# Gathered second product four tokens wide, with a ring of nine buffers, in an encoder layer with a mixture of small experts

## Chip, core and metric

One core of a Trainium2 chip runs the whole program in one launch. The metric is the device time of the launch in microseconds, the median of three runs. The engines of the core are TensorE (PE in the rows; PEld is its weight load), VectorE (DVE), ScalarE (ACT), GpSimd (POOL) and SyncE (SP); each executes its own instructions in the order in which they were built into the program, and waits on semaphores for the others. SP, ACT and POOL issue transfers to 16 DMA engines, which they share.

## What is computed

One encoder layer is applied to a prompt of 256 tokens and a sample of 1024, both 1024 features wide, in float32. Two branches (a gated linear recurrence and a latent attention) are merged and added to the input. Then each token picks 128 of 16384 experts (8 heads, the 16 best of each), and its output is the sum over its experts:

```python
u = jnp.take(u_tab, eidx, axis=0)
ve = jnp.take(v_tab, eidx, axis=0)
act = jax.nn.gelu(jnp.einsum('td,thkd->thk', zt, u).astype(jnp.float32), approximate=False) * g
return jnp.einsum('thk,thkd->td', act.astype(zt.dtype), ve)
```

Here `zt` is the normed token, `g` the softmax over its picks. A closing norm follows. `u_tab` and `v_tab` have 16384 rows of 1024 float32 numbers, 4 KB a row.

## The kernel before

Tokens go by tiles of 128. There are two prompt tiles and eight sample tiles. For six of the ten tiles (both of the prompt, the sample's first two, `r0`, and its last two, `r1`) the experts' rows are gathered; for the four sample tiles between them (`ND` = 512 tokens) all 16384 experts are computed, those not picked with weight zero (`dense`).

A gathered tile takes 256 gathers. One gather brings 128 rows, one to each partition, 512 KB in all, as an indirect DMA issued by GpSimd.

- First product (`u_steps`, L933 and L935): gather s brings every token's row of its slot s; VectorE multiplies it by the normed token `zs` and sums over the features (`dots`). 128 gathers a tile. Behind them come the gelu and the weights (`act`).
- Second product by tokens (`v_steps`, L946 to L978), for the prompt's tiles and the sample's first: gather t brings all 128 rows of one token, and TensorE contracts them over the partitions with that token's activations. The activations are transposed first (L949). A token t = 32 g + i writes into column group g of the array (`tile_position=(0, g_ * 32)`) and adds into its own row of `acc`; the weights are zero in the other 31 columns (`zt`). Each token takes two matmuls of 512 columns, and two tokens of neighbouring groups are handed over together (`VG = 2`).
- Second product by slots (`v_slots`, L989 and L991), for `r0[1]` and both of `r1`: gather s brings every token's row of slot s, and VectorE multiplies it by the activation and adds it to `vacc`.

All these rows land in one ring of five buffers of 4 KB a partition (`tag="ring", bufs=5`), in the order in which they are asked for; the n-th gather waits until VectorE or TensorE is through with the gather five before it. The two vectors `gfin` and `gffn`, gains of the closing norm and of the norm in front of the experts, lie in buffers of their own, loaded once.

`experts(routes)` interleaves a tile's first product with the second product of the tile before it, one step each in turn. It is called for the two prompt tiles while the sample's projection, recurrence and attention run, and for `r0 + r1` while the rest of the sample's attention, its merge and then `dense` run.

The stages around it are `attn_core` for the sample (L138 `kt,qt`, L618, L624), `merge` for the sample's first two tiles and then the other six (wo products, L140 `msh,wh`; wq products, L138 `xg,wraw`; the picks on VectorE in `best` and `half`, closed by a transpose in `finish_picks`, L892 or L912), `weights` (L1024, L1043) and `dense`. `dense` walks over 128 blocks of 128 experts: `first(b)` loads a block of u, splits it in two float32r parts (`uh` on ScalarE, `ul` on VectorE, L124), makes three products for each of 8 slices (L140 to L142, `zth,uh`), a gelu, a multiplication by the picks' weights (`ge`, L1072), and a split of the result; `second(g)` does the same with v for four blocks at a time (`vl`, L124), and VectorE adds the products to `acc` (L1086).

The order of instructions on each engine isn't written out by hand. The framework's scheduler sets it when the program is built, from dependencies, priorities and a simulated timeline (`schedule_with_timeline_sim=True`); the steps of the second products are issued with high priority. `dense` and `experts` are written one after the other, and the scheduler merges them. Part of each partition's memory is set aside for the descriptors of transfers that GpSimd issues, 16384 bytes unless said otherwise.

Of the kernel before, what the change touches and what calls it, by code (L numbers as in the profile page):

```python
# [12 lines left out]
F32 = mybir.dt.float32  # L13
# [25 lines left out]
VG = 2  # L39
# blocks of the input projection, 128 columns each  # L40
B_Q, B_FF, B_FB, B_I, B_G, B_CQ, B_CKV, B_GLH, B_GLA, B_PE = 0, 4, 8, 12, 16, 20, 23, 25, 33, 41
# columns of the gains
# [8 lines left out]
def encoder(ctx, tc, I, O, dbg=None):  # L51
# [10 lines left out]
    # ---------------------------------------------------------------- constants  # L62
# [21 lines left out]
    # lower bounds: softmax over the two rows, first row  # L84
# [33 lines left out]
    # ---------------------------------------------------------------- helpers  # L118
# [8 lines left out]
    # Operands of the large products come either whole, as (x,) in float32, or split exactly in two  # L127
    # float32r parts, as (high, low).
# [25 lines left out]
    def put(dst, src):  # L154
        # dst: the parts of src
        if len(dst) == 1:
            nc.scalar.copy(dst[0], src)
        else:
            nc.scalar.copy(dst[0], src)  # L159
            nc.vector.tensor_tensor(dst[1], src, dst[0].bitcast(F32), op=OP.subtract)  # L160

    def rsqrt_to(pool, out, src, inv_n, shape, name, vy=None):
        # (src * inv_n + EPS) ** -0.5, one Newton step on exp(-ln/2)
# [9 lines left out]
    def rsqrt_small(pool, out, src, inv_n, shape, name):  # L173
        # the same on VectorE alone, for a few elements: three Newton steps from the exponent's half
# [11 lines left out]
    def norm_T(pool, xs, nk, n, name, bank, fold=False):  # L186
        # xs: [128, n] each, features on partitions; rsqrt of the mean square, on all partitions
# [15 lines left out]
    # ---------------------------------------------------------------- input projection  # L203
    def project(s0, S, ap, wpool, bank, np_, whole):
        """Norm, then blocks of the projection into DRAM; a generator, so that users of the blocks
        can be put between them."""
# [83 lines left out]
    # ---------------------------------------------------------------- HGRN2, one head  # L290
# [3 lines left out]
    def prefixes(hp, f, n, dirs, tg, nb):  # L294
        """From forget gates [P, len(dirs), n] (0 backward, 1 forward): inputs' gates in place of f, prefixes of
        the logarithms inside chunks (backward exclusive, forward inclusive), and the chunks' totals."""
# [26 lines left out]
    def xexp(hp, fb, tot, di, t0, comp, tag):  # L323
        # exp of the prefix, or of what is left to the chunk's end
# [12 lines left out]
    def hgrn_states(s0, S, h, dirs, hp, nb, bank):  # L337
        """States at the chunks' starts."""
# [42 lines left out]
    def hgrn_out(s0, S, h, t0, hp, nb, bank, pre=None):  # L381
        """Outputs of LS tokens: scores inside chunks, level by level, and the states' share."""
# [83 lines left out]
    # ---------------------------------------------------------------- attention  # L466
# [11 lines left out]
    def attn_prep(s0, S, bp, wpool, bank, va, spill):  # L478
        """Latents' norms, then values, and per head keys and queries; these two go to DRAM when spill is set."""
# [8 lines left out]
        for dst, b0, nk, gc in ((ck, 0, 2, G_KVA), (cq, 3, 3, G_QA)):  # L488
# [6 lines left out]
            else:  # L495
                # read into the low part, and split there
# [5 lines left out]
        # keys' rotary part, shared by the heads  # L502
# [13 lines left out]
        # values, token on partitions  # L516
# [41 lines left out]
    def attn_core(s0, nk, q0s, cp, va, keys, queries, bankS, bankT, bankO):  # L558
        """Softmax and values for two heads and QG queries at a time."""
# [95 lines left out]
    # ---------------------------------------------------------------- merge and routing  # L655
    NC_ = 80

    def candidates(cp, vals, top, pos, h0):
        """Best 16 sums of 4 heads. With both lists sorted, the sum of ranks (i, j) has (i + 1)(j + 1) - 1 others
        before it, so that ranks 0 x 16, 1..7 x 8 and 8..15 x 1 hold all of the best; they stay in their order."""  # L660
# [18 lines left out]
    def ranks(cp, pos):  # L679
        # (i, j) of a candidate's place  # L680
# [18 lines left out]
    def merge(s0, t0, G, nd, routes, wpool, rp, bank, wb=3, small=False, tbank=None, tside="left", tctx=None, cut=0, sp=None, mp=None):  # L699
        """Merge, residual and picks of G tokens, of which the first nd tiles' experts are all taken,  # L700
        the others' gathered. Products go by segments of tokens;
        cut: 1 splits the operands of the output's products, 2 those of the branches' too."""
        with ExitStack() as own, ExitStack() as cctx:
# [10 lines left out]
            with ExitStack() as mctx:  # L714
# [39 lines left out]
                def rows(k, x2):  # L754
                    # rows of the residual, and the sum of squares
# [45 lines left out]
            def norm():  # L801
                # what the scores are a factor short of
# [9 lines left out]
            def half(c, hf):  # L812
                # picks of 4 heads: weights and ids
# [72 lines left out]
            def finish_picks(c):  # L886
# [8 lines left out]
                else:  # L895
                    # With an id's halves as 8 (a + 8) + c, and A, C those of a number, 1 - (a - A) ** 2 - (c - C) ** 2
                    # is 1 where they are equal and less than 1 elsewhere; codes are the rows of this product that
                    # belong to the id: 8 a, c, a ** 2 + c ** 2 and 1, small integers all of them.
# [18 lines left out]
            # one half of the dense tiles' picks, and of the first tile's, is done by now  # L917
# [6 lines left out]
    # ---------------------------------------------------------------- experts  # L924
    def u_steps(route):
        tt, gw, ei = route["tt"], route["gw"], route["ei"]
        zs = pe_.tile([P, D], F32, name="zs", tag="zs")
        nc.gpsimd.dma_start(zs, x2d[tt:tt + P])
        nc.vector.scalar_tensor_tensor(out=zs, in0=zs, scalar=route["rt"], in1=gffn, op0=OP.mult, op1=OP.mult)
        dots = pe_.tile([P, P], F32, name="dots", tag="dots", bufs=2)  # L930
        for s in range(P):
            ug = pe_.tile([P, D], F32, name="ug", tag="ring", bufs=5)
# [13 lines left out]
    def v_steps(route):  # L946
# [5 lines left out]
        for b in range(4):  # L952
            # a token's activations in its own column, zeros beside it
            zt = zts[0]
            o = (b + 3) % 4 * 8
# [26 lines left out]
    def v_slots(route):  # L982
# [4 lines left out]
        for s in range(P):  # L987
# [4 lines left out]
            if s % 2:  # L992
                yield
        sq = pe_.tile([P, D], F32, name="sq", tag="ring", bufs=5)
        finish(acc, sq, tt)
        yield

    def finish(y, sq, tt):
# [311 lines left out]
```

## Time and profile before

| | |
|---|---|
| median of 3 runs | 4386.39 us (4372.38 to 4390.8) |
| span of the profiled execution | 4377.9 us |
| TensorE busy | 4002.2 us (91%) |
| VectorE busy | 3375.4 us (77%) |
| GpSimd busy | 1840.3 us (42%) |
| ScalarE busy | 1571.5 us (36%) |
| moved by DMA | 1258.09 MB, mean 287 GB/s |

The profile is one execution of the program. Its span runs from the first to the last instruction and is 8.5 us shorter than the median of the timed runs. A busy share is an average over stages that have different limits, so the stages are read apart below. Ends of matmuls are modelled: the time of one is better read from start to start. The record of a gathered row's operation on VectorE at L935 is double (the operation and the read of its accumulator).

### The profile page before, as it was taken

Reading aid. Unit: us, or ns where it says so; the run is one execution under the profiler, and the core shown is the slowest. Engines: PE = TensorE matmul, PEld = TensorE weight load, DVE = VectorE, ACT = ScalarE, POOL = GpSimd, SP = SyncE. Lnnn points to the kernel's source line nnn. Section 1 sums busy time; section 2 is a strip of 40 time slices with the busy share of each in tenths; the row PEclk is TensorE's granted clock in tenths of the full one; section 3 lists DMA queues with packets and bytes.
Section 4 is the critical chain, followed back from the end, with each engine's and each line's share of the span. In section 5 each row is a group of like instructions: output and inputs, shape, how many; then the busy total and the mean of one; then the engine's idle time right before and its main releaser. Section 6 shows DMA issues by size and latency. Waiting matters only on the chain.

```text
span 4377.9 us, 54156 instructions
## 1 busy us (share of the span) xinstructions
PE 4002.2 (91%) x17693; PEld 2741.6 (63%) x17693; DVE 3375.4 (77%) x8088; ACT 1571.5 (36%) x2608; POOL 1840.3 (42%) x1565
## 2 busy tenths in 40 slices
PE   7998999998888999976999949999999999999994
PEld 6787778664434652334654404678888888888883
DVE  4637977466877675388668887869999899999997
ACT  6554474453233213332210117843332233233221
POOL 0000644333444233366445552335555455555554
PEclk9999999999999999988999969999999999999997
DMA  5364999888889877699778776889999999999996
GB/s 166 120 198 132 344 337 332 293 271 282 283 288 308 296 242 265 217 309 351 276 264 277 269 268 224 313 309 341 336 330 341 318 344 343 348 326 354 327 320 230
DMA packets 506731, 1258.09 MB, mean 287 GB/s; under 512 B 49744, under 2 KB 202960, under 8 KB 504400
## 3 DMA queue, kind: packets, MB, share of 16 engines
q0 software_dynamic: 224352, 816.94, 53.3%
q1 hardware_dynamic: 195472, 348.29, 23.5%
q10 hardware_dynamic: 86624, 89.40, 6.0%
q8 instruction: 140, 2.29, 0.2%
q14 instruction: 143, 1.17, 0.1%
HBM read 1159.29 MB, written 95.16 MB: 287 GB/s over the span
## 4 chain that ended last, share of the span: by engine, by line
PE 67%; DMA 10%; DVE 8%; issue 8%; ACT 4%; POOL 3%; POOLq 0%; ACTq 0%; SPq 0%; DVEq 0%
PE pm L140 14%; PE pm L141 14%; PE pm L142 14%; PE pm L138 9%; PE acc L970 7%; DMA ug<-peer_u,ei 5%; DMA vg<-peer_v,eit 3%; PE pm L1043 3%; DVE ug L935 2%; POOL ug L933 2%; PE pm L437 1%; POOL vg L963 1%; PE pm L1024 1%; PE pm L624 1%; PE pm L618 1%
## 5 line engine op out<-in xcount | busy, mean ns | idle before, releaser
L933 POOL DMA_INDIRECT ug<-peer_u,ei x768 | 913.0, 1189 | 915.1 <-DVE ug L935 362.8
L935 DVE SCALAR_TENSOR_TENSOR ug<-ug,zs 128x1024 f32<-128x1024 f32 x768 | 931.6, 1219 | 172.7 <-DMA ug<-peer_u,ei 147.5
L989 POOL DMA_INDIRECT vg<-peer_v,ei x384 | 508.0, 1323 | 454.0 <-DVE vacc L991 280.0
L963 POOL DMA_INDIRECT vg<-peer_v,eit x384 | 404.9, 1055 | 659.1 <-PE acc L970 368.9
L970 PE MATMUL acc<-vg,zt 128*32 128x512 f32 x1536 | 551.5, 643 | 117.6 <-DMA vg<-peer_v,eit 116.0
L991 DVE SCALAR_TENSOR_TENSOR vacc<-vg,act,vacc 128x1024 f32<-128x1024 f32 x384 | 490.9, 1278 | 24.5 <-DMA vg<-peer_v,ei 23.2
L140 PE MATMUL pm<-zth,uh 128*128 128x512 f32 x1024 | 405.2, 396 | 2.4 <-ACT gs L1044 2.0
L142 PE MATMUL pm<-zth,ul 128*128 128x512 f32 x1024 | 405.2, 396 | 0.0
L141 PE MATMUL pm<-ztl,uh 128*128 128x512 f32 x1024 | 404.7, 395 | 0.0
L141 PE MATMUL pm<-vl,ah 128*128 128x512 f32 x1024 | 398.8, 392 | 0.0
L140 PE MATMUL pm<-vh,ah 128*128 128x512 f32 x1024 | 392.4, 393 | 6.1 <-ACT ah L159 3.7
L142 PE MATMUL pm<-vh,al 128*128 128x512 f32 x1024 | 391.6, 392 | 0.0
L970 PEld LDWEIGHTS acc<-vg,zt 128*32 128x32 f32 x1536 | 95.2, 112 | 399.1 <-issue 213.5
L123 ACT CAST vh<-vraw 128x512 fp32r<-128x512 f32 x256 | 157.5, 619 | 445.9 <-DMA vraw<-peer_v 389.6
L138 PE MATMUL pm<-xg,wraw 128*128 128x256 f32 (+1 forms) x1024 | 293.9, 437 | 0.0
L140 PE MATMUL pm<-hh,wh 128*128 128x512 f32 x672 | 268.9, 400 | 5.1 <-ACT gt L255 4.5
L141 PE MATMUL pm<-hl,wh 128*128 128x512 f32 x672 | 267.0, 397 | 0.0
L142 PE MATMUL pm<-hh,wl 128*128 128x512 f32 x672 | 266.3, 396 | 0.0
L123 ACT CAST uh<-uraw 128x1024 fp32r<-128x1024 f32 x128 | 134.6, 1051 | 365.1 <-PE pm L141 344.2
L138 PEld LDWEIGHTS pm<-xg,wraw 128*128 128x128 f32 x1024 | 189.8, 192 | 81.5 <-issue 64.5
L140 PEld LDWEIGHTS pm<-vh,ah 128*128 128x128 f32 x1024 | 193.0, 188 | 50.6 <-ACT ah L159 4.6
L140 PEld LDWEIGHTS pm<-zth,uh 128*128 128x128 f32 x1024 | 192.6, 188 | 49.3 <-ACT gs L1044 2.2
(368 smaller groups left out, 7583.8 us busy)
## 6 DMA issues: line engine op xcount, KB each, us to landing
uraw<-uT SPq DMA_DIRECT2D x128, 512.0 KB, 7.0
vraw<-peer_v SPq DMA_DIRECT2D x256, 256.0 KB, 6.3
wraw<-wi SPq DMA_DIRECT2D x84, 512.0 KB, 4.2
gd<-gs ACTq DMA_DIRECT2D x16, 2048.0 KB, 9.5
g<-gd ACTq DMA_DIRECT2D x32, 1024.0 KB, 18.6
wraw<-wq SPq DMA_DIRECT2D x48, 512.0 KB, 4.0
wraw<-wo SPq DMA_DIRECT2D x24, 512.0 KB, 4.9
ug<-peer_u,ei POOLq DMA_INDIRECT x768, 6.5
```

What stands on the lines that cost most here:

```text
L123: nc.scalar.copy(hi, src)
L138: nc.tensor.matmul(out, w[0], x[0], start=start, stop=stop)
L140: nc.tensor.matmul(out, w[0], x[0], start=start, stop=False)
L141: nc.tensor.matmul(out, w[0], x[1], start=False, stop=False)
L142: nc.tensor.matmul(out, w[1], x[0], start=False, stop=stop)
L933: nc.gpsimd.indirect_dma_start(out=ug, out_offset=None, in_=I["peer_u"], in_offset=bass.IndirectOffsetOnAxis(ap=ei[:, s:s + 1], axis=0))
L935: nc.vector.scalar_tensor_tensor(out=ug, in0=ug, scalar=1.0, in1=zs, op0=OP.mult, op1=OP.mult, accum_out=dots[:, s:s + 1])
L963: nc.gpsimd.indirect_dma_start(out=vg, out_offset=None, in_=I["peer_v"], in_offset=bass.IndirectOffsetOnAxis(ap=eit[:, t:t + 1], axis=0))
L970: nc.tensor.matmul(acc[g_ * 32:(g_ + 1) * 32, n * 512:(n + 1) * 512], zt[:, g_, i], v_[:, n * 512:(n + 1) * 512], start=b == 0 and i == 0, ...
L989: nc.gpsimd.indirect_dma_start(out=vg, out_offset=None, in_=I["peer_v"], in_offset=bass.IndirectOffsetOnAxis(ap=ei[:, s:s + 1], axis=0))
L991: nc.vector.scalar_tensor_tensor(out=acc, in0=vg, scalar=act[:, s:s + 1], in1=acc, op0=OP.mult, op1=OP.add)
L1043: nc.tensor.matmul(pm[:, j * P:(j + 1) * P], ol[:, j], oh[:, j], start=True, stop=True)
```

## The change

1. The ring has nine buffers (`RING = 9`) instead of five. Every tile in it is taken by `ring(name)`.
2. `v_steps` hands over four tokens at a time, one of each column group, instead of two. Since four rows of weights are now in use together, the zeroed weights `zt` have two halves, and the activations are written for 4 times 4 tokens, eight times a tile, instead of 4 times 8, four times a tile.
3. `gfin` and `gffn` have no buffers of their own any more. Each use loads its vector into a buffer of the ring, on SP's queue: `gffn` once per gathered tile, `gfin` once per gathered tile and once for the dense ones.
4. The memory for descriptors is 8192 bytes a partition instead of 16384.
5. Comments are taken out. Nothing else of the program's text is changed.

```diff
-VG = 2
+RING = 9

+    def ring(name):
+        return pe_.tile([P, D], F32, name=name, tag="ring", bufs=RING)
+
     def u_steps(route):
...
         nc.gpsimd.dma_start(zs, x2d[tt:tt + P])
+        gffn = ring("gffn")
+        nc.sync.dma_start(gffn, I["norm_ffn"].partition_broadcast(P))
...
-            ug = pe_.tile([P, D], F32, name="ug", tag="ring", bufs=5)
+            ug = ring("ug")
...
-        for b in range(4):
-            # a token's activations in its own column, zeros beside it
-            zt = zts[0]
-            o = (b + 3) % 4 * 8
-            nc.vector.memset(ap_of(zt[:, 0, 0, o:o + 1], [[256, 4], [33, 8]]), 0.0)
-            nc.vector.tensor_copy(ap_of(zt[:, 0, 0, b * 8:b * 8 + 1], [[256, 4], [33, 8]]), actT[:, :, b * 8:b * 8 + 8])
-            for i in range(8):
+        zt = zts[0]
+        for b in range(8):
+
+            h = b % 2
+            o = (b + 6) % 8 * 4
+            nc.vector.memset(ap_of(zt[:, h, 0, 0, o:o + 1], [[128, 4], [33, 4]]), 0.0)
+            nc.vector.tensor_copy(ap_of(zt[:, h, 0, 0, b * 4:b * 4 + 1], [[128, 4], [33, 4]]), actT[:, :, b * 4:b * 4 + 4])
+            for i in range(4):
                 vgs = []
                 for g in range(4):
-                    t = g * 32 + b * 8 + i
-                    vg = pe_.tile([P, D], F32, name="vg", tag="ring", bufs=5)
+                    t = g * 32 + b * 4 + i
+                    vg = ring("vg")
...
-                    vgs.append((g, vg))
-                    if len(vgs) == VG:
-                        # neighbours in different columns of the array run side by side
+                    vgs.append(vg)
+                    if g == 3:
+
                         for n in range(2):
-                            for g_, v_ in vgs:
-                                nc.tensor.matmul(acc[g_ * 32:(g_ + 1) * 32, n * 512:(n + 1) * 512], zt[:, g_, i],
+                            for g_, v_ in enumerate(vgs):
+                                nc.tensor.matmul(acc[g_ * 32:(g_ + 1) * 32, n * 512:(n + 1) * 512], zt[:, h, g_, i],
...
+    def final_gain():
+        gfin = ring("gfin")
+        nc.sync.dma_start(gfin, I["norm_final"].partition_broadcast(P))
+        return gfin
+
-    def finish(y, sq, tt):
+    def finish(y, sq, tt, gfin=None):
+        gfin = final_gain() if gfin is None else gfin
...
-    gfin = pe_.tile([P, D], F32, name="gfin")
-    nc.sync.dma_start(gfin, I["norm_final"].partition_broadcast(P))
-    gffn = pe_.tile([P, D], F32, name="gffn")
-    nc.sync.dma_start(gffn, I["norm_ffn"].partition_broadcast(P))
-    zts.append(pe_.tile([P, 4, 8, 32], F32, name="zt0"))
+    zts.append(pe_.tile([P, 2, 4, 4, 32], F32, name="zt0"))
...
-    nc = _bacc.Bacc("TRN2", target_bir_lowering=False, num_devices=1)
+    nc = _bacc.Bacc("TRN2", target_bir_lowering=False, num_devices=1, dynamic_dma_scratch_size=8192)
```

The scheduler makes a new order of all engines from this. Two places are shown. The first is TensorE while the sample's attention runs beside a second product (`acc<-vg` is one matmul of a token's half; `kt,qt` are attention scores, `ident,pn` transposes of probabilities, `ps,vs` the values' product). Before:

```order
L970 MATMUL acc<-vg,zt_3902 32x512 x3
L624 MATMUL pm<-ps,vs 64x256 x2
L618 MATMUL pm<-ident,pn 128x128 x4
L970 MATMUL acc<-vg,zt_3902 32x512
L624 MATMUL pm<-ps,vs 64x256 x2
L618 MATMUL pm<-ident,pn 128x128 x3
L970 MATMUL acc<-vg,zt_3902 32x512 x3
L618 MATMUL pm<-ident,pn 128x128
L138 MATMUL pm<-kt,qt 128x512
L970 MATMUL acc<-vg,zt_3902 32x512
```

TensorE, the changed kernel, at the like place:

```order
L976 MATMUL acc<-vg,zt_3898 32x512
L138 MATMUL pm<-kt,qt 128x512 x2
L624 MATMUL pm<-ps,vs 64x256 x2
L618 MATMUL pm<-ident,pn 128x128 x2
L976 MATMUL acc<-vg,zt_3898 32x512
L138 MATMUL pm<-kt,qt 128x512
L618 MATMUL pm<-ident,pn 128x128 x2
L976 MATMUL acc<-vg,zt_3898 32x512 x5
```

Before, the first matmul of a pair stands by itself and the other three together; after, the first matmuls of three tokens stand by themselves, then the fourth token's first and the four second halves.

The second place is VectorE in the dense stage, at the 43rd block (`ug,dots` is a gathered row's operation of the first product; `ge` is the multiplication by the picks' weights, one a block; `ul` and `vl` are the splits of u and v; `al` that of the result). Before:

```order
L1072 TENSOR_TENSOR ge<-ge,g 128x512
L935 SCALAR_TENSOR_TENSOR ug,dots<-ug,zs 128x1024 x2
L124 TENSOR_TENSOR ul<-uraw,uh 128x1024
L1072 TENSOR_TENSOR ge<-ge,g 128x512
L935 SCALAR_TENSOR_TENSOR ug,dots<-ug,zs 128x1024
L160 TENSOR_TENSOR al<-ge,ah 128x512
L124 TENSOR_TENSOR vl<-vraw,vh 128x512
L935 SCALAR_TENSOR_TENSOR ug,dots<-ug,zs 128x1024
L160 TENSOR_TENSOR al<-ge,ah 128x512
L935 SCALAR_TENSOR_TENSOR ug,dots<-ug,zs 128x1024
L124 TENSOR_TENSOR vl<-vraw,vh 128x512
L935 SCALAR_TENSOR_TENSOR ug,dots<-ug,zs 128x1024
```

VectorE, the changed kernel, at the same block:

```order
L940 SCALAR_TENSOR_TENSOR ug,dots<-ug,zs 128x1024 x2
L1082 TENSOR_TENSOR ge<-ge,g 128x512
L124 TENSOR_TENSOR ul<-uraw,uh 128x1024
L124 TENSOR_TENSOR vl<-vraw,vh 128x512
L1082 TENSOR_TENSOR ge<-ge,g 128x512
L940 SCALAR_TENSOR_TENSOR ug,dots<-ug,zs 128x1024 x3
L124 TENSOR_TENSOR ul<-uraw,uh 128x1024
L124 TENSOR_TENSOR vl<-vraw,vh 128x512
L940 SCALAR_TENSOR_TENSOR ug,dots<-ug,zs 128x1024 x6
L124 TENSOR_TENSOR ul<-uraw,uh 128x1024
L124 TENSOR_TENSOR vl<-vraw,vh 128x512
L940 SCALAR_TENSOR_TENSOR ug,dots<-ug,zs 128x1024
```

Behind two `ge` there stand single gathered rows between the splits before, and groups of three and six after.

## Rows read from the trace of the kernel before

**Rows 1.** Stretches: from:to, length, busy PE PEld DVE ACT POOL, clock, DMA share, GB/s.
```profile
435.00:785.00 350.00, 336.60 (x1573) 277.30 (x1571) 286.76 (x693) 181.62 (x251) 165.04 (x136) 0.99 0.94 339
785.00:1473.00 688.00, 620.21 (x2601) 348.15 (x2601) 494.69 (x1252) 254.59 (x415) 265.09 (x256) 0.97 0.86 287
1473.00:1837.00 364.00, 353.62 (x1518) 157.93 (x1517) 190.61 (x849) 98.03 (x217) 123.86 (x128) 0.99 0.75 247
1837.00:2099.00 262.00, 201.05 (x935) 116.29 (x935) 218.94 (x411) 82.97 (x180) 170.01 (x134) 0.84 0.92 322
2099.00:2697.00 598.00, 517.79 (x1987) 255.73 (x1986) 444.89 (x1808) 121.76 (x190) 281.80 (x254) 0.92 0.78 268
2697.00:2885.00 188.00, 174.53 (x1027) 114.54 (x1025) 143.00 (x280) 160.05 (x222) 44.61 (x44) 0.96 0.75 277
2885.00:4317.00 1432.00, 1425.00 (x6140) 1155.24 (x6141) 1308.84 (x1747) 427.61 (x646) 763.45 (x587) 1.00 0.94 333
4317.00:4378.00 61.00, 1.13 (x5) 0.58 (x4) 42.07 (x87) 5.75 (x10) 24.84 (x22) 0.53 0.58 206
```

**Rows 2.** The line that transposes activations: count, min/median/max ns, first and last start.
```profile
L949 PE MATMUL acc<-ident,act x3: 270/270/272, 780.0 to 2099.2; 128*128 128x128 f32 x3
```

**Rows 3.** Stretches, columns as above: best 25 us, picks, middle of the dense stage.
```profile
550.00:575.00 25.00, 23.86 (x107) 19.35 (x105) 17.68 (x38) 13.40 (x16) 10.58 (x9) 1.00 1.01 372
...
2509.00:2627.00 118.00, 61.78 (x138) 13.09 (x136) 96.74 (x444) 15.14 (x26) 66.24 (x55) 0.71 0.79 266
3000.00:4000.00 1000.00, 999.57 (x4323) 810.94 (x4322) 926.33 (x1285) 303.70 (x460) 540.31 (x416) 1.00 0.95 337
```

**Rows 4.** Waits, dense stage, DVE and POOL: us in total, times, longest.
```profile
DVE vacc L991 <- DMA vg<-peer_v,ei: 16.2, 18, 2.8
DVE ug L935 <- DMA ug<-peer_u,ei: 14.4, 14, 3.1
...
POOL vg L989 <- DVE vacc L991: 253.6, 165, 9.5
```

**Rows 5.** Timeline of PE: start, us; a float32 matmul of this line leaves two records.
```profile
861.51 1.04 PE L970 MATMUL acc<-vg,zt 128*32 128x512 f32 x2
...
866.12 1.90 PE L970 MATMUL acc<-vg,zt 128*32 128x512 f32 x6
...
1632.46 1.93 PE L970 MATMUL acc<-vg,zt 128*32 128x512 f32 x14
```

**Rows 6.** Timeline of PE: wq products and a transpose of ids.
```profile
1631.93 0.60 PE L138 MATMUL pm<-xg,wraw 128*128 128x256 f32 x2
...
1671.29 0.33 PE L892 MATMUL pm<-ident,ids 128*128 128x128 f32 x1
...
2254.56 3.60 PE L138 MATMUL pm<-xg,wraw 128*128 128x512 f32 x8
```

**Rows 7.** Waits of PE, 785 to 1473 us and then 2099 to 2697 us.
```profile
PE acc L970 <- DMA vg<-peer_v,eit: 41.0, 21, 5.0
...
PE acc L970 <- DMA vg<-peer_v,eit: 64.7, 29, 5.5
```

**Rows 8.** Stretches, tile ug alone: busy DVE and POOL, clock, DMA share, GB/s.
```profile
2500.00:2600.00 100.00, 28.30 (x46) 23.92 (x22) 0.73 0.78 264
```

**Rows 9.** DMA issues of the page: count, KB each, median us to landing.
```profile
uraw<-uT SPq DMA_DIRECT2D x128, 512.0 KB, 7.0
vraw<-peer_v SPq DMA_DIRECT2D x256, 256.0 KB, 6.3
...
g<-gd ACTq DMA_DIRECT2D x32, 1024.0 KB, 18.6
```

**Rows 10.** Groups of the page: busy us, mean ns; idle before, releaser.
```profile
L935 DVE SCALAR_TENSOR_TENSOR ug<-ug,zs 128x1024 f32<-128x1024 f32 x768 | 931.6, 1219 | 172.7 <-DMA ug<-peer_u,ei 147.5
...
L991 DVE SCALAR_TENSOR_TENSOR vacc<-vg,act,vacc 128x1024 f32<-128x1024 f32 x384 | 490.9, 1278 | 24.5 <-DMA vg<-peer_v,ei 23.2
```

**Rows 11.** Timeline of DVE: the last rows' operations.
```profile
4349.21 2.61 DVE L991 SCALAR_TENSOR_TENSOR vacc<-vg,act,vacc 128x1024 f32<-128x1024 f32 x2 [0.26 <-DMA vg<-peer_v,ei]
```

More of the change, by code (lines that the diff above doesn't have):

```diff
@@ L966, in v_steps @@
-                    if len(vgs) == VG:
+                    vgs.append(vg)
+                    if g == 3:
                         for n in range(2):
-                            for g_, v_ in vgs:
-                                nc.tensor.matmul(acc[g_ * 32:(g_ + 1) * 32, n * 512:(n + 1) * 512], zt[:, g_, i],
+                            for g_, v_ in enumerate(vgs):
+                                nc.tensor.matmul(acc[g_ * 32:(g_ + 1) * 32, n * 512:(n + 1) * 512], zt[:, h, g_, i],
                                                  v_[:, n * 512:(n + 1) * 512], start=b == 0 and i == 0,
-                                                 stop=b == 3 and i == 7, tile_position=(0, g_ * 32), skip_group_check=True)
-                        vgs = []
+                                                 stop=b == 7 and i == 3, tile_position=(0, g_ * 32), skip_group_check=True)
@@ L974, in v_steps @@
                     yield
-        y = pe_.tile([P, D], F32, name="y", tag="ring", bufs=5)
-        x2r = pe_.tile([P, D], F32, name="x2r", tag="ring", bufs=5)
+        y = ring("y")
+        x2r = ring("x2r")
         nc.gpsimd.dma_start(x2r, x2d[tt:tt + P])
@@ L987, in v_slots @@
         for s in range(P):
-            vg = pe_.tile([P, D], F32, name="vg", tag="ring", bufs=5)
+            vg = ring("vg")
             nc.gpsimd.indirect_dma_start(out=vg, out_offset=None, in_=I["peer_v"],
@@ L993, in v_slots @@
                 yield
-        sq = pe_.tile([P, D], F32, name="sq", tag="ring", bufs=5)
-        finish(acc, sq, tt)
+        finish(acc, ring("sq"), tt)
         yield
-    def finish(y, sq, tt):
+    def final_gain():
[4 more added lines that the diff above has]
+        gfin = final_gain() if gfin is None else gfin
         ss = pe_.tile([P, 1], F32, name="fss", tag="fss")
@@ L1095, in dense @@
             second(g)
+        gfin = final_gain()
         for t, r in enumerate(routes):
-            sq = pe_.tile([P, D], F32, name="sq", tag="ring", bufs=5)
-            finish(acc[:, t], sq, r["tt"])
+            finish(acc[:, t], ring("sq"), r["tt"], gfin)
     def experts(routes):
```

## Prediction

> **What bounds the kernel now.** I cut the span into stages at events of TensorE and read each with the table of stretches [rows 1]: 0 to 785 us (up to the first gathered second product, at the transpose of the first tile's activations [rows 2]), 785 to 1473 (first prompt tile's second product beside the second tile's first), 1473 to 1837 (second prompt tile's second product alone), 1837 to 2099 (first product of the first sample tile, up to the last of the three transposes [rows 2]), 2099 to 2697 (that tile's second product beside the next tile's first), 2697 to 2885 (weights of the dense tiles), 2885 to 4317 (the dense stage), and the tail. The reader is to see two things. TensorE is busy for nearly all of each, except 1837 to 2099 (201 of 262 us) and around the dense tiles' picks (62 of 118 us at 2509 [rows 3]). And in the dense stage two limits stand level: TensorE 1425 of 1432 us, DMA 0.94 with 333 GB/s, 337 GB/s in its middle thousand us [rows 3]. The waits there agree: VectorE waits only 14 + 16 us for gathered rows, while GpSimd's gathers wait 254 us for a buffer that VectorE has not yet left [rows 4]. The gathers run as fast as VectorE's order lets them, and that order happens to ask for what the DMA engines can bring.
>
> **The four-wide product.** One product is 1.04 us by itself, three are 1.90 us, seven are 1.93 us where four column groups overlap [rows 5]; so four groups do run side by side. But in the built order of before, a product rarely meets its partner: 112 stand in groups that cost one pass and 175 in groups that cost two (a few more), 112 x 1.04 + 175 x 1.90 = 449 us. In the changed order the first half of A, B and C is started as soon as each row is there, and only D meets others (D0, A1, B1, C1, D1: two passes, because D occurs twice): 200 groups of one pass and 93 of two, 208 + 177 = 385 us. TensorE saves 64 us, all of it before the dense stage. The Trainium skill (TensorEngine Tiling (Array Packing), Theoretical Speedup) gives up to 4x for a small dimension of 32. An estimate by that page would be 768 x 1.04 / 4 = 200 us, a saving of 249 us instead of 64; the seven products agree with it, the order does not give it the chance.
>
> **Where the dense stage starts.** The 64 us do not come out at its start, because the scheduler put the work elsewhere. Stage by stage, TensorE's work counted from the built order with the prices above, 0.23 us for a float32r product of 512 columns (1432 us for 6144 [rows 1]) and 0.90 us for a float32 one (3.60 us for four [rows 6]):
> 1. To the first gathered product: TensorE's order has 63 us less ahead of it (643 instead of 706), but it needs 128 gathered rows, and DMA was already at 0.94 and 339 GB/s here [rows 1]. Between 745 and 785; I take 765.
> 2. First tile: order 571 instead of 612 us; 256 gathers are 134 MB, and the other traffic is 287 GB/s x 688 us - 134 = 63 MB [rows 1], together 197 MB, 588 us at the 335 GB/s of the two fullest stages; with waits on rows like those before, 41 us [rows 7]: 625 (588 to 688) instead of 688.
> 3. Second tile alone: order 300 instead of 357 us, and before came within 2% of it: 310 (300 to 340) instead of 364.
> 4. The sample's first product: 128 gathers, 262 us before at 0.92 DMA [rows 1]. Two things change. The picks of these tokens now end right behind the second tile's last product, while before their transpose (L892) was done at 1671 us, 166 us ahead of it; this puts some 40 us in front, from the last wq products at 1632 to L892 [rows 6]. And TensorE has 82 us of attention to do in this stretch, 168 before: it stands still until the rows are through. The rows are 67 MB, the other traffic was 17 MB, of which I leave half here: 75 MB at 335 GB/s, 224 + 40 = 265 (240 to 290).
> 5. Next tile: order 510 us (attention that was in stage 4 before), waits before 65 us on rows [rows 7]: 575 (530 to 640) instead of 598.
> 6. To the dense stage: 302 us of work instead of 159. The wq products of the dense tiles now end behind the last gathered product (100 us), the picks then have no cover (VectorE was busy 97 of 118 us there [rows 3], 28 of 83 us on gathered rows [rows 8] that are no longer there: 75 us), and the weights all stand behind (202 us of work; before took 188 for 159: 239). 415 (380 to 450) instead of 188.
> Sum: 765 + 625 + 310 + 265 + 575 + 415 = 2955 us, 70 later than 2885.
>
> **The dense stage.** This decides. I counted in VectorE's built order how many of the gathered rows' operations (L935 and L991, L940 and L996 after) stand between the blocks' multiplications by the weights (L1072, L1082). Before, 558 of 1152 stand ahead of block 1, then 35 to 39 per eight blocks to the end, 4.4 a block. After, 591 ahead of block 1, then about 60 per eight blocks, all gone by block 78: 561 in 77 blocks, 7.3 a block, then none. The scheduler counts on the deeper ring to bring rows faster; in fact the DMA engines are full. VectorE works in order, so each splitting of weights (ul, vl) that stands behind a row waits for it, and TensorE for the split. Traffic of these 77 blocks: 561 x 0.524 MB = 294 MB, weights of u and v 77 x 1.05 = 81 MB, gate blocks 19 x 1.05 = 20 MB [rows 9], 395 MB. At 341 GB/s, a little over the 337 of the middle thousand because the queue is never short, it takes 1160 us. Bounds: 372 GB/s, the best 25 us of before [rows 3], gives 1062; the gathers' pace of before, 411 rows in 1000 us or 2.43 us each, gives 1363. The Trainium skill (DMA: Bandwidth & Descriptors, Specifications) puts the HBM limit of a core at about 358 GB/s. An estimate by that page would be 1103 us; the stretch with 372 GB/s lies above it, so the row is the bound. VectorE itself would be busy 561 x 1.25 [rows 10] + 77 x 4.6 = 1055 us, so it is near its limit too (4.6: 926 us less 411 x 1.25, over 89 blocks [rows 3]). The other 51 blocks run without gathers at TensorE's pace, 1432 / 128 = 11.2 us: 571. Dense: 1160 + 571 = 1731, not 1432.
>
> **The rest.** The end after the last product: the gathers' tail is gone (61 us [rows 1]), what stays is the closing norm, 26 us from the last row's operation to the end of the span [rows 11]. The gains' loads on SP's queue (13 instead of 2) wait for a ring buffer, and the loads of u and v queue behind: nothing where those run a block ahead, up to 12 us each for the five in the dense stage; I take zero and keep 60 above. The smaller descriptor memory: no row shows it; at most it holds the gathers to the old pace, which is a rival. The two memsets of 4 for one of 8 are nothing on VectorE.
>
> Sum: 2955 + 1731 + 26 = 4712 us of span. Before has 4378 of span in the profiled execution and a median of 4386; with these 8 us, 4720.
>
> **Rivals.**
> 1. Faster: the rows come as fast as the order asks, since nine buffers hide the landing. For: gathers wait for buffers, not for data [rows 4]. Then TensorE keeps 1432 us, the front end gains its 64: 2821 + 1432 + 26 + 8 = 4287. It decides from 42 MB per eight blocks in 90 us, 474 GB/s; the best stretch is 372. 5%.
> 2. Crowded, but both ends at their best: front 2821, 395 MB at 372 GB/s: 1062, then 571 and 34: 4488. 12%.
> 3. The clock: TensorE has work for 862 of the 1160 us, and where it was busy 77% its granted clock was 0.84 and at 52% 0.71 [rows 1, 3]. At 0.74 nothing is added, at 0.65 of full speed the crowded stage is 1326 us: 4886. 8%.
> 4. The change doesn't do what it says: the ring is no faster (descriptor memory, or another wait), 2.43 us a row, 1363 for 1160: 4923. 8%.
> 5. Four-wide doesn't overlap: a run of five costs three passes, 93 x 0.9 = 84 us more before the dense stage: 4804. Inside the range; 6%.
> 6. No change: the front end would have to gain some 260 us more than I give it; only a stage 4 and 6 without stalls comes near. 3%.
>
> **Numbers.** The forecast has 58%. The range 4480 to 4890 takes in rivals 2, 3 and 5, and the bounds of the stages. Faster by over 0.5% (about what a measurement of this kernel can tell from no change) 5%, within 0.5% 3%, slower 92%.
>
> **What would show it.** In the changed profile: the crowded stage with TensorE near 75% busy, waiting for splits, DMA at 0.95 or over, and VectorE's largest wait on gathered rows; gathers ended near block 78, some 570 us before the end; a last stretch with TensorE full and DMA low. TensorE idle for over 100 us ahead of the third L954. Wrong would be: TensorE full in the whole dense stage (rival 1), or a dense start far from 2955.

## The result and the profile after

The changed kernel takes 4590.38 us (median of 4 runs) against 4382.52 us of the kernel before on the same chip: ratio 1.0479, 95% interval 1.0456 to 1.0501. It is slower by 208 us. Its profiled execution spans 4596.9 us, the one of before 4377.9.

First the stretches of the changed kernel, cut at the same events as [rows 1] and with the same columns; the crowded part of the dense stage and the part behind it stand in two rows.

```profile
435.00:750.00 315.00, 285.48 (x1271) 231.48 (x1271) 274.34 (x676) 161.43 (x223) 176.99 (x139) 0.95 0.95 350
750.00:1392.00 642.00, 586.71 (x2483) 340.15 (x2483) 448.75 (x1098) 237.96 (x383) 272.85 (x255) 0.96 0.87 301
1392.00:1701.00 309.00, 294.13 (x1494) 167.64 (x1498) 191.04 (x856) 64.01 (x129) 124.24 (x127) 0.98 0.92 321
1701.00:1930.00 229.00, 109.43 (x425) 48.46 (x417) 208.01 (x462) 62.34 (x140) 168.03 (x137) 0.67 0.93 333
1930.00:2454.00 524.00, 506.02 (x2325) 264.62 (x2324) 321.60 (x845) 134.23 (x265) 282.57 (x250) 0.98 0.88 311
2454.00:2889.00 435.00, 350.36 (x1653) 221.27 (x1649) 364.96 (x1427) 234.99 (x334) 77.17 (x72) 0.85 0.49 181
2889.00:4000.00 1111.00, 930.03 (x3622) 716.23 (x3622) 1048.00 (x1355) 257.55 (x384) 740.83 (x575) 0.92 0.98 367
4000.00:4581.00 581.00, 580.67 (x2522) 472.96 (x2521) 286.20 (x412) 178.84 (x268) 0.97 (x2) 1.00 0.37 115
4581.00:4597.00 16.00, 0.75 (x4) 0.29 (x2) 8.97 (x36) 2.03 (x4) 1.76 (x4) 0.65 0.32 131
```

The dense stage starts at 2889, 4 us later than before; it lasts 1692 us instead of 1432; the tail is 16 instead of 61. 4 + 260 - 45 = 219, the whole difference of the spans. In the first 1111 us of the dense stage VectorE (94% busy) and the DMA engines (share 0.98) are full and TensorE (84%) is not; GpSimd is busy for 67% and waits for the rest, mostly for buffers. In the next 581 us TensorE is full and the other three have little to do. The work was not made more (1152 gathered rows in both kernels), it was heaped up. Below, "the heap" is this first part, the crowded stage of the prediction.

The waits inside the heap, 2889 to 4000 us: first those of TensorE, then VectorE's on gathered rows, then GpSimd's largest (us in total, times, longest).

```profile
PE pm L141 <- DVE vl L124: 102.9, 38, 6.2
PE pm L140 <- ACT vh L123: 24.6, 13, 4.7
PE pm L140 <- DVE acc L1096: 22.2, 17, 4.8
...
DVE vacc L996 <- DMA vg<-peer_v,ei: 3.3, 3, 1.5
...
DVE ug L940 <- DMA ug<-peer_u,ei: 1.0, 1, 1.0
...
POOL vg L994 <- DVE vacc L996: 144.0, 104, 15.0
```

TensorE waits for the low halves of the weights (vl), which VectorE writes. VectorE hardly waits for rows (4 us): it is busy for 1048 of 1111 us, and GpSimd stands behind it. Its groups in that stretch:

```profile
L996 DVE SCALAR_TENSOR_TENSOR vacc<-vg,act,vacc 128x1024 f32<-128x1024 f32 x337 | 431.8, 1281 | 6.9 <-DMA vg<-peer_v,ei 3.3
L940 DVE SCALAR_TENSOR_TENSOR ug<-ug,zs 128x1024 f32<-128x1024 f32 x235 | 282.7, 1218 | 1.0 <-DMA ug<-peer_u,ei 1.0
```

These are 572 rows, 714 us of VectorE. What TensorE lost can be split with the two dense rows: 2522 products in 580.67 us are 0.230 us each at clock 1.00, so the 3622 of the heap are 834 us of work. 1111 - 930 = 181 us are waits, and 930 - 834 = 96 us are products that took longer. The granted clock averaged 0.92 there, which would make 906 us of the 834: an estimate of some 72 us for the clock. The other 24 us no row separates.

### The profile page after: what moved, and what is told of

Same layout as the page of the kernel before. It is cut to its first block, busy times and chain, and to the rows that moved or that the text cites. A ratio compares the mean times of both kernels' runs of the same rounds, so it can differ in the third digit from the quotient of the medians.

```text
span 4596.9 us, 54383 instructions
## 1 busy us (share of the span) xinstructions
PE 4019.8 (87%) x17693; PEld 2782.4 (61%) x17693; DVE 3395.0 (74%) x8112; ACT 1570.6 (34%) x2602; POOL 1846.1 (40%) x1565
## 5 line engine op out<-in xcount | busy, mean ns | idle before, releaser
L938 POOL DMA_INDIRECT ug<-peer_u,ei x768 | 939.3, 1223 | 773.9 <-DVE ug L940 252.0
L994 POOL DMA_INDIRECT vg<-peer_v,ei x384 | 485.1, 1263 | 320.9 <-DVE vacc L996 209.2
L141 PE MATMUL pm<-vl,ah 128*128 128x512 f32 x1024 | 431.7, 422 | 103.1 <-DVE vl L124 102.9
L976 PE MATMUL acc<-vg,zt 128*32 128x512 f32 x1536 | 420.5, 613 | 24.5 <-DMA vg<-peer_v,eit 24.5
L142 PE MATMUL pm<-vh,al 128*128 128x512 f32 x1024 | 422.4, 414 | 0.0
L141 PEld LDWEIGHTS pm<-vl,ah 128*128 128x128 f32 x1024 | 207.5, 203 | 167.3 <-DVE vl L124 123.2
L140 PEld LDWEIGHTS pm<-vh,ah 128*128 128x128 f32 x1024 | 202.3, 199 | 122.5 <-DVE acc L1096 36.3
L1096 DVE TENSOR_TENSOR acc<-pm,acc 128x512 f32<-128x512 f32 x256 | 171.5, 685 | 109.1 <-PE pm L142 107.9
```

Of the source, the lines that this page charges most:

```text
L140: nc.tensor.matmul(out, w[0], x[0], start=start, stop=False)
L141: nc.tensor.matmul(out, w[0], x[1], start=False, stop=False)
L142: nc.tensor.matmul(out, w[1], x[0], start=False, stop=stop)
L938: nc.gpsimd.indirect_dma_start(out=ug, out_offset=None, in_=I["peer_u"], in_offset=bass.IndirectOffsetOnAxis(ap=ei[:, s:s + 1], axis=0))
L976: nc.tensor.matmul(acc[g_ * 32:(g_ + 1) * 32, n * 512:(n + 1) * 512], zt[:, h, g_, i], v_[:, n * 512:(n + 1) * 512], start=b == 0 and i == ...
L994: nc.gpsimd.indirect_dma_start(out=vg, out_offset=None, in_=I["peer_v"], in_offset=bass.IndirectOffsetOnAxis(ap=ei[:, s:s + 1], axis=0))
```

## Experiments

Three theories were set against each other. A: the deeper ring makes the scheduler pack the gathered rows closer in VectorE's order, and VectorE, in whose order the weights' splits stand behind the rows, is the limit. B: the DMA engines are the limit, as I had predicted. C: the four-wide product and its order cost the time. "Rows a block" below is counted in VectorE's built order, per block of the dense stage.

### Which part of the change costs the time

Two tokens wide with nine buffers:

```
-                    vgs.append(vg)
-                    if g == 3:
+                    vgs.append((g, vg))
+                    if len(vgs) == 2:
...
+                        vgs = []
```

> The changed kernel with the gathered second product two tokens wide again; the ring of nine, the norm vectors on demand and the half descriptor memory stay. In VectorE's built order the gathered rows stand as close as in the changed kernel (591 ahead of block 1, 1152 by block 81: 7 a block). Theory A (ring): nine buffers make the scheduler put the rows that close, VectorE's work there is 4.9 + 1.28 x 7 = 13.9 us a block, over the 11.2 of TensorE; so the crowded stage stays near 1110 us for 80 blocks, the dense stage near 1690, and the time is that of the changed kernel or up to 70 us more: 4590 to 4660. Rival C (width): the four-wide product and its order lose the time; then this kernel comes back to 4380 to 4420.

Measured: 4701.19 us, ratio 1.0735 (1.0698 to 1.0772). C falls: without the wide product it is slower still. The dense stage runs from 2986 to 4685, 1699 us, as long as in the changed kernel. The start lies 97 us later, which puts the time 41 us above the range that A gave.

Then the same with `RING = 5`, so that the vectors on demand and the smaller descriptor memory alone are left:

> Two-wide and a ring of five, so that only the norm vectors on demand, the shared tags and the half descriptor memory are left of the change. Built order: 559 rows ahead of block 1, then 35 to 40 per eight blocks, 1117 by block 128, as before. Theory A: dense stage 1432 us and the time of before within 1%, 4360 to 4420. Rival D (the on-demand vectors or the smaller descriptor memory cost the time): 4500 or more.

Measured: 4387.92 us, ratio 1.0022 (1.0006 to 1.0037). Dense stage 2897 to 4330, 1433 us. These two parts cost 8 us (3 to 16 by the interval). From five to nine buffers the two-wide kernel loses 313 us in the medians and 305 in the profiled spans (start +89, dense +266, tail -49), and the width gives 111 back.

### The heap taken apart, with the rest of the change kept

Nine buffers as in the changed kernel, but split under two tags; from the first stage whose products are accumulated on VectorE only `LATE` of them are used:

```
...
+        turn[0] += 1
+        if turn[1] == RING and turn[0] % RING >= LATE:
+            return pe_.tile([P, D], F32, name=name, tag="ring2", bufs=RING - LATE)
+        return pe_.tile([P, D], F32, name=name, tag="ring", bufs=LATE)
...
+            if prev and "acc" in prev:
+                turn[1] = LATE
```

> All of the change is kept, four-wide and nine buffers, but from the point at which products are accumulated on VectorE (the second half of the last stages, 5 tiles of steps before the end) only five of the nine buffers are handed out. Built order: 564 rows ahead of block 1, 1124 by block 128, 4.4 a block. Theory A: VectorE needs 4.9 + 1.28 x 4.4 = 10.5 us a block, TensorE 11.2, so the dense stage is 1432 us again; with a start at 2890 and a tail of some 50 us for the rows left over: 4360 to 4390. Rival C (width): 4560 to 4600, as the changed kernel. Rival B (DMA alone is the limit, as I predicted): (1.31 + 0.524 x 4.4) MB a block at 341 GB/s is 10.6 us, so it also gives a full TensorE; this run does not tell A from B.

Measured: 4353.42 us, ratio 0.9929 (0.9908 to 0.9950). Start 2857, dense 1435 us, 52 us behind it. The dense stage is the one that A and B both give; the start is 33 us earlier than assumed, so the time lies just under the range.

> As the run with five late buffers, with six. Built order: 568 rows ahead of block 1, 1126 by block 113, all gone before the end, 5.0 a block. Theory A: VectorE 4.9 + 1.28 x 5.0 = 11.3 us a block, level with TensorE; dense 1435 to 1460, no tail of rows: 4340 to 4380. Rival B: 3.93 MB a block at 341 GB/s is 11.5 us, 4370 to 4400. Rival C: 4560 to 4600.

Measured: 4324.17 us, ratio 0.9872 (0.9836 to 0.9909). The dense stage is 1493 us, longer than either theory said, and the start at 2810, 80 us earlier than I had assumed, makes up for it. While the rows last:

```profile
2810.00:4180.00 1370.00, 1326.39 (x5611) 1056.51 (x5612) 1274.06 (x1681) 400.05 (x599) 752.98 (x594) 0.99 0.96 346
```

VectorE is busy for 93% and TensorE for 97%. The theories' sums take the larger of the engines' times and leave out the waits between them; TensorE's are 44 us here.

With the rows beside the dense stage held at 4.4 or 5 a block, the loss is gone and a small gain is left. That gain is not the change's alone: the split into two tags altered the order of the front end too (TensorE's gathered products take 362 and 361 us in these two kernels, 420.5 in the changed one), and no run has the split without the cap.

### VectorE or DMA

The changed kernel with half of VectorE's work per late row:

```
...
+            w = D // 2 if late else D
-            nc.vector.scalar_tensor_tensor(out=ug, in0=ug, scalar=1.0, in1=zs, ...
+            nc.vector.scalar_tensor_tensor(out=ug[:, :w], in0=ug[:, :w], scalar=1.0, in1=zs[:, :w], ...
...
+            w = D // 2
-            nc.vector.scalar_tensor_tensor(out=acc, in0=vg, ...
+            nc.vector.scalar_tensor_tensor(out=acc[:, :w], in0=vg[:, :w], ...
...
```

> The changed kernel, but from the point at which products are accumulated on VectorE, VectorE works only on the first 512 of the 1024 columns of each gathered row (the other half of those sums is left out); the gathers bring the same bytes. Built order: 598 rows ahead of block 1, 1107 by block 65, all by about block 69, 8 a block. Theory A (VectorE is the limit of the crowded stage, DMA has room): a row costs about 0.65 us, 4.9 + 0.65 x 8 = 10.1 us a block, under TensorE's 11.2; dense 1435 to 1480, time 4330 to 4400. Theory B (the DMA engines, at a share of 0.98 there, are level with VectorE): (1.31 + 0.524 x 8) MB a block at the 367 GB/s of that stage is 15.0 us, 69 blocks take 1035 us and the other 59 another 661: dense 1696, time 4560 to 4620 as before the cut, and VectorE's largest wait is on gathered rows, over 200 us.

Measured: 4591.9 us, one run; nothing gained. Dense stage 2903 to 4575, 1672 us. Its stretches (columns as above), then the largest waits of VectorE and of TensorE, 2889 to 3900 us:

```profile
3100.00:3300.00 200.00, 169.72 (x648) 128.68 (x647) 146.77 (x309) 45.60 (x72) 121.87 (x115) 0.91 1.01 395
3300.00:3500.00 200.00, 169.30 (x656) 127.89 (x655) 144.39 (x251) 46.23 (x71) 125.33 (x118) 0.93 1.01 393
3500.00:3700.00 200.00, 167.83 (x657) 128.38 (x656) 140.80 (x299) 45.28 (x68) 117.67 (x113) 0.94 1.01 391
3700.00:3900.00 200.00, 166.36 (x621) 126.46 (x620) 147.03 (x211) 43.72 (x66) 131.26 (x120) 0.89 1.02 400
3900.00:4100.00 200.00, 200.00 (x867) 162.70 (x866) 109.44 (x164) 65.84 (x101) 2.68 (x3) 1.00 0.46 148
```

```profile
DVE acc L1100 <- PE pm L142: 93.8, 33, 8.4
DVE ul L124 <- ACT uh L123: 64.0, 24, 13.8
DVE vacc L1000 <- DMA vg<-peer_v,ei: 43.6, 55, 1.8
DVE ug L943 <- DMA ug<-peer_u,ei: 20.2, 25, 1.8
...
PE pm L141 <- DVE vl L124: 73.9, 29, 6.8
PE pm L140 <- issue: 32.5, 20, 4.8
```

VectorE now has over a quarter of its time free, the DMA engines are at a share of 1.01 and 391 to 400 GB/s, and TensorE keeps the same busy share (0.84). A, which said that VectorE alone held the stage, falls. The time is B's, the waits are not: VectorE waits 64 us on rows, not over 200, and its two largest waits are on TensorE's products and ScalarE's split. What stands is that the rows' order asks more than either engine can give in a block's 11.2 us: 4.9 + 1.28 x 7 = 13.9 us of VectorE and 1.31 + 0.524 x 7 = 5.0 MB, 13.6 us at 367 GB/s. That the DMA engines are the limit once VectorE's excess is gone is argued from their share and the unchanged time, not shown: queues that wait for one another in order are a rival here. The order grew closer here too (8 rows a block for 7), and the opposite test, fewer bytes in an order as close, was not run.

### How deep the ring may be

`RING = 8` and `RING = 7`, nothing else:

> The changed kernel with a ring of eight. Built order: 583 rows ahead of block 1, 993 by block 65, 1101 by block 81, all by about block 89: 6.5 a block. Theory A: 4.9 + 1.28 x 6.5 = 13.2 us a block for 88 blocks, 11.2 for 40: dense 1610, with a start at 2890 and a tail of 16: 4500 to 4550. Theory B: 4.7 MB a block at 367 GB/s is 12.8 us, 4470 to 4500. If depth as such did not matter (rival C, width), 4580 to 4600.

Measured: 4476.43 us, one run. The time lies in B's range, but by the start: it is 2824, not the 2890 that I had put in. The dense stage, 1635 us, is longer than A's 1610 and B's 1574 (12.8 us for 88 blocks, 11.2 for 40).

> The changed kernel with a ring of seven, nothing else. Built order: 577 rows ahead of block 1, 1110 by block 97, 5.55 a block, all by about block 105; and on TensorE no query product of the dense tiles is left between the last gathered product and the weights, as with eight (130 are in the changed kernel). VectorE: 4.9 + 1.28 x 5.55 = 12.0 us a block for 104 blocks, 11.2 for 24: dense 1517. Start as with eight buffers, 2824, tail 16: 4340 to 4375, within 1% under the kernel before. If the start depends on the number of buffers itself, not on what is left in TensorE's queue, it lies at 2860 to 2885 as with five: 4390 to 4420.

Measured: 4392.32 us, ratio 1.0016 (1.0002 to 1.0031), the upper of the two times. Yet the start was 2828, as the first theory had it; the dense stage was 1553 us, 36 more than the sum of VectorE's work. So the time lies in the second theory's range, but not for its reason.

### The width, and where else the last rows could go

> The run with six late buffers, two tokens wide. Built order in the dense stage the same (568 ahead of block 1, 1125 by block 113, 5.0 a block). If the four-wide product is worth what the two runs with nine buffers show (dense start 2889 instead of 2986), the dense stage starts some 97 us later than in the four-wide kernel: 4410 to 4430. If it is worth only its busy time (485 - 420 = 65 us): 4380 to 4395.

Measured: 4464.29 us, ratio 1.0180 (1.0150 to 1.0209). Above both expectations: the start is 2958 instead of 2810, so the width is worth 148 us at the start here; the table below shows what stands in front of it. The dense stage is as long (1488 and 1493 us).

```
-    for r in r0[1:] + r1:
+    for r in r1:
         r["acc"] = vp
-    experts(r0 + r1)
+    experts(r0)
+    experts(r1)
```

> Six late buffers, and the second product of the second sample tile goes through TensorE like those of the first three tiles, ahead of the first product of the last two tiles (before it was accumulated on VectorE beside the dense stage). 128 rows leave VectorE (164 us), TensorE gets 512 more small products (about 420 / 3 = 140 us, less what they find of the 85 idle us ahead of the dense stage). Built order: 543 rows ahead of block 1, 1016 of 1024 by block 97, 5.0 a block. Theory A: the dense stage is no shorter, since TensorE sets it; the start moves back by 55 to 140 us: 4380 to 4470, slower than the kernel with six late buffers. Rival (the rows beside the dense stage are what costs): 4300 or less.

Measured: 4394.24 us, one run: start 2899, dense 1478. As expected, no gain: the start is 89 us later than with six late buffers and the dense stage only 15 us shorter. The order kept its 5 rows a block to block 97, so this run does not tell what those rows cost beside the dense stage.

### Two kernels from what was found

> Four-wide, eight buffers, five of them in the last stages. Built order: 563 rows ahead of block 1, 1123 by block 128, 4.4 a block; 16 query products left behind the last gathered product. Start 2825 to 2835, dense 1435 and tail 51 as with nine and five: 4305 to 4335. If the start does not follow the products left: 2857 as with nine and five, 4350.

Measured: 4270.33 us, ratio 0.9748 (0.9732 to 0.9764): 2.5% under the kernel before and 7% under the changed one, the best of all. Start 2783 (some 40 us earlier than expected, hence a time below the range), dense 1427 us.

> Four-wide, seven buffers, six of them in the last stages. Built order: 571 rows ahead of block 1, 1128 by block 113, 5.0 a block; no query product left. Start 2815 to 2830, dense 1493 and tail 16 as with nine and six: 4320 to 4345. If six late buffers are no better than seven, 4340 to 4375.

Measured: 4304.99 us, ratio 0.9821 (0.9800 to 0.9843). Start 2803, dense 1484 us; both are a little shorter than expected, and the time lies below the range.

The dense stage of the kernel with eight and five, in the columns above, and its TensorE waits, 2783 to 4209 us:

```profile
2783.00:4000.00 1217.00, 1213.09 (x5241) 983.28 (x5240) 1112.21 (x1526) 368.40 (x556) 636.70 (x498) 1.00 0.94 337
4000.00:4209.00 209.00, 208.29 (x903) 169.28 (x902) 196.51 (x220) 59.45 (x90) 113.31 (x89) 1.00 0.91 317
```

```profile
PE pm L141 <- ACT ah L160: 2.2, 1, 2.2
PE pm L141 <- ACT gs L1061: 1.6, 1, 1.6
```

TensorE full to the end, clock 1.00, DMA at 0.94 and 337 GB/s: the picture of [rows 3], 102 us earlier.

### All runs in two tables

The dense stage against the rows a block:

| kernel | rows a block | dense, us |
|---|---|---|
| eight, five late, four-wide | 4.4 | 1427 |
| five, two-wide, the kernel before | 4.4 | 1432 |
| five, two-wide | 4.4 | 1433 |
| nine, five late, four-wide | 4.4 | 1435 |
| nine, six late, four-wide, a tile moved to TensorE | 5.0 | 1478 |
| seven, six late, four-wide | 5.0 | 1484 |
| nine, six late, two-wide | 5.0 | 1488 |
| nine, six late, four-wide | 5.0 | 1493 |
| seven, four-wide | 5.55 | 1553 |
| eight, four-wide | 6.5 | 1635 |
| nine, four-wide (the change) | 7 | 1692 |
| nine, two-wide | 7 | 1699 |

Width and front end have next to no say in it: at the same rows a block the dense stages lie within 15 us. The run with half of VectorE's work (8 rows a block, 1672 us) is not in the table, since its rows cost less.

In every run of the table the rows a block follow the number of late buffers (five 4.4, six 5.0, seven 5.55, eight 6.5, nine 7), so no run has the order without the depth. A rival is that nine buffers delay the loads of the weights by themselves. The traces speak against it; from issue to landing, in us, before (3000 to 4000 us) and in the heap:

```profile
uraw<-uT SPq DMA_DIRECT2D x88, 512.0 KB, 7.0
vraw<-peer_v SPq DMA_DIRECT2D x186, 256.0 KB, 6.5
```

```profile
uraw<-uT SPq DMA_DIRECT2D x78, 512.0 KB, 6.8
vraw<-peer_v SPq DMA_DIRECT2D x147, 256.0 KB, 6.6
```

The start against what stands on TensorE behind the last gathered product (query products of the dense tiles, counted in the built order, before the picks and the 1024 weight products):

| kernel | last gathered product, us | query products behind it | dense start, us |
|---|---|---|---|
| seven, six late | 2565 | 0 | 2803 |
| seven | 2569 | 0 | 2828 |
| eight | 2508 | 0 | 2824 |
| eight, five late | 2473 | 16 | 2783 |
| nine, six late | 2472 | 56 | 2810 |
| nine, five late | 2453 | 128 | 2857 |
| nine (the change) | 2455 | 130 | 2889 |
| nine, two-wide | 2509 | 176 | 2986 |
| nine, six late, two-wide | 2495 | 184 | 2958 |

The two kernels with five buffers throughout and the one with the moved tile are left out: there a part of the weight products already stands ahead of the last gathered one. Nine buffers end the gathered products first, but leave the most query products behind them, and by and large the more are left, the longer it is from the last gathered product to the dense stage (238 to 316 us with none, 404 to 477 with 128 or more). The count is not the whole account: nine with five late and the changed kernel have nearly the same count and lie 32 us apart; from 2454 us to the dense stage TensorE is busy 326 us at a mean clock of 0.90 in the first and 350 us at 0.85 in the second. In the changed kernel and in the one with eight and five (TensorE's groups, 2454 to 2889 us and 2460 to 2783 us; the second begins 13 us ahead of the last gathered product):

```profile
L138 PE MATMUL pm<-xg,wraw 128*128 128x256 f32 (+1 forms) x260 | 87.3, 488 | 0.0
L871 PE MATMUL pm<-kj,qT 128*128 128x128 f32 x100 | 16.2, 299 | 15.2 <-ACT qT L867 15.2
L912 PE MATMUL pm<-ident,gw 128*128 128x128 f32 x4 | 1.8, 454 | 43.8 <-DVE gw L827 43.8
```

```profile
L139 PE MATMUL pm<-xg,wraw 128*128 128x256 f32 (+1 forms) x61 | 20.2, 484 | 2.8 <-DVE sr L856 2.8
L872 PE MATMUL pm<-kj,qT 128*128 128x128 f32 x24 | 3.7, 292 | 1.7 <-ACT qT L868 1.7
L913 PE MATMUL pm<-ident,gw 128*128 128x128 f32 x4 | 1.8, 454 | 53.8 <-DVE gw L828 53.8
```

119 us of query work against 28 (busy and waits); in both TensorE then stands still for the picks, 44 and 54 us. Why the orders differ in how much they leave stays open.

## Why the prediction was right, and where it was not

The forecast was 4720, slower, and the time 4590 lies in the range. The span was forecast 115 us too long (4712 against 4597): 66 at the front, 39 in the dense stage, 10 in the tail. Point by point:

**The reading of the order** was right, and it is what carried the forecast: some 7 rows a block to about block 78, then none. On the chip 1148 of the 1152 rows ran ahead of the 79th multiplication by the weights, at 4005, and the last one at 4012. The 571 us for the rest were 569 us, from 4012 to 4581.

**The size of the crowded stage** was wrong by 37 us: 1160 against 1123 (2889 to 4012). The term that failed is the 341 GB/s. [Rows 1, 3] show five buffers, and their rate was what VectorE's order asked for, as the prediction itself says of GpSimd's waits; I still took it for what the engines can bring. With nine the stretch has 367. At that rate my 395 MB are 1076 us, close to the 1055 that I had worked out for VectorE: the two limits that I set against each other were level. That the miss is 37 us and not 84 is a second error, the other way: by 4000 us the stretch had moved 408 MB (367 GB/s x 1111 us), not 395.

**The mechanism** was half right. "The DMA engines are full" holds (0.98), but VectorE's largest wait was to be on gathered rows, and it waited 4 us for them: with 94% of its time busy, VectorE's own work was a limit too. Halving that work left the time the same, with the DMA engines 7 to 9% higher (391 to 400 GB/s); which of the two binds in the changed kernel no run separates. A prediction with VectorE's 1055 us as the bound would have come out 68 us short of the 1123, no nearer, but it would have told what to look for: waits of GpSimd on VectorE.

**TensorE in the crowded stage** was busy 84%, not 75%, at a clock of 0.92; the rival of a slower clock (0.65) did not come, but of the 277 us lost there some 72 are clock, by the estimate above.

**The front end** was 66 us too long: 750, 642, 309, 229, 524 and 435 us against 765, 625, 310, 265, 575 and 415. Two terms were too long, those of the fourth and the fifth stage. The 40 us in front of the sample's first product were charged for the picks' transpose; but the gathers need only `ei`, which is written in two halves. The conversion and the gathers in the trace of the changed kernel, 1500 to 1760 us:

```profile
L938 POOL DMA_INDIRECT ug<-peer_u,ei x37: 937/973/1973, 1686.4 to 1760.0; - x37
L845 DVE CAST ei<-ids x2: 186/190/195, 1653.8 to 1755.5; 128x64 int32<-128x64 f32 x2
```

The first 64 columns were there at 1654 and the gathers ran from 1686, while TensorE waited for `ids` (56 us, no loss); 75 MB at the 333 GB/s of that stretch are 225 us, and it took 229. TensorE idle for over 100 us ahead of the third transpose held: 120 of 229. The other term is the waits on rows in the second and the fifth stage, 41 and 65 us, kept from [rows 7]: with nine buffers they are 9 and 8. The second stage was 17 us longer than forecast all the same: TensorE was busy 587 us there, not 571, and waited 46 us for other things.

```profile
L954 PE MATMUL acc<-ident,act x3: 272/272/273, 749.7 to 1930.0; 128*128 128x128 f32 x3
L976 PE MATMUL acc<-vg,zt 128*32 128x512 f32 x1536 | 420.5, 613 | 24.5 <-DMA vg<-peer_v,eit 24.5
```

**The product.** The saving of 64 us was the width's (485.0 in the two-wide kernel with nine buffers, 420.5 here, 65 less). That they agree to 1 us is luck: both sums that it was the difference of were short (449 and 385), and with six late buffers the width takes off 91 (451.7 and 360.8). The ring took off another 66 (551.5 before), which I had not priced. That the saving does not come out at the start of the dense stage held, and for the reason given: the query products and the bare picks. Yet with the order of eight and five the dense stage does start 102 us earlier than before.

**The edits costed at nothing** (vectors on demand, descriptor memory) were 8 us together, 3 to 16 by the interval.

**The tail** was 16 us, not 26.

## What to carry to other kernels

A deeper buffer ring under a scheduler is not only more cover for latency: it changes how much of each engine's in-order queue the ring's users take, so count, per unit of the main work, how many of their operations stand ahead of it, and compare both the engine's time and the bytes with that unit's time. Use the depth where the ring's users are the main work, and cap it where they are the background (here 5 beside the dense stage, 8 ahead of it: -2.5% instead of +4.8%). A rate read in a stretch where the requester was held back is a lower bound for the engine, not its limit.

## What the runs showed of the hardware

The rate of the DMA engines at a full share was not one number: 337 GB/s at 0.95 in the dense stage of before [rows 3], 367 at 0.98 in the changed kernel, 391 to 400 at 1.01 and 1.02 over stretches of 200 us with half of VectorE's work. Why the rate rose, no run here tells apart.

The Trainium skill (HBM Reference, Specifications (TRN2)) says that a core streaming alone gets well above its 358 GB/s share of the memory, about 425 GB/s. The 391 to 400 GB/s here lie above the share too, which agrees; no run here reaches 425. The 358 that the prediction cites as a limit is none for this kernel on one core.

In the stretch from 1701 to 1930 us of the changed kernel TensorE was busy 109 of 229 us and its granted clock averaged 0.67, so that it had the lower of its two levels (1.2 and 2.4 GHz) for a part of the time; from 435 to 750 it was busy 285 of 315 and averaged 0.95. The dense stage shows the same pair: 84% busy with a mean of 0.92 in the heap, full with the upper level throughout (1.00) behind it.
